# A two-block transformer kernel: order of the first loads, of two matmul halves, and the queue of three small loads

## The chip, the cores and the metric

One of the eight cores of a Trainium2 chip runs the whole program. The metric is the device time of one execution in microseconds. Engines are named as the profile names them: PE (TensorE, with PEld for its weight loads), ACT (ScalarE), DVE (VectorE), POOL (GpSimd), SP (SyncE, which here only issues transfers).

## The reference

Two transformer blocks follow one another on x of 256 tokens by 1024 features, float32. What matters here is the start of the first one:

```
def first_block(x, mem, positions, g_norm, w_in, ...):
    cos_a, sin_a = rope_tables(positions, A_ROT)
    cos_b, sin_b = rope_tables(positions, B_ROPE)
    for layer in range(DEPTH):
        h = rms_norm(x, g_norm[layer])
        proj = h @ w_in[layer]
        (q_a, k_a, v_a, q_i, k_i, w_i, z_a, c_q, c_kv, k_rope, z_b, q_m, z_m,
         gate_logits) = jnp.split(proj, split_at, axis=-1)
...
```

The projection feeds three attention branches (sparse top-k, latent, and cross attention to `mem`), each gated and projected, and a sum with x. The second block has a mixer (differential attention and gated linear attention), cross attention, and a mixture of 32 experts in 4 groups with two experts per token; the experts' weights alone are 201 MB.

## The kernel before, in words

**Products.** Every dense product is a `Job`: a matrix of weights cut in blocks of 128 rows, and up to 512 columns. `ORDER` (line 31) lists by hand in which order the jobs' halves (four blocks of rows each) are loaded and multiplied; it begins `c1 c2 c2 c1`, which are two parts of 336 columns each of `w_in`. `Stream` (line 102) walks through that list. `fetch` (line 128) takes a piece of memory and issues the load of the next half on SP's queue; `top_up` (line 146) fetches as long as fewer than `room` (6 at the start) loads are in flight and pieces are free. `split` (line 161) cuts a load into units of two blocks of rows (four for narrow products) and makes two float32r parts of each unit: ACT rounds it (line 165, the high part), DVE takes the remainder (line 166, the low part). `pump` (line 189) splits up to four units ahead and then issues a unit's matmuls (line 214).

**Three matmuls per block.** The left side, x transposed, is also kept as a high and a low part (`Left`, line 55). For each block `i` and each half `t` of the tokens, `pump` issues three matmuls, `c` = 0, 1, 2. Line 213 chooses the part of x, line 214 the part of the weights:

```
steps = [(i, t, c) for i in range(kb) for t in range(NT) for c in range(3)]
if 0:
    steps.sort(key=lambda s_: s_[2] == 2)
...
    x_ = j.X.at(k0 + off + i)[c == 0][:, t * P:(t + 1) * P]
    mm(j.outs[t], lhsT=x_, rhs=hl[:, int(c == 2), i, :], ...)
```

Index 0 is the high part, 1 the low part. So c = 0 is low x by high weights, c = 1 high by high, c = 2 high x by low weights.

**The start.** Lines 415 to 433 issue the first loads, all on SP's queue, in this order: columns 0 to 511 of x (512 KB, `load_x(0)`), the positions (line 421), three gain vectors (`g_norm`, `g_cq`, `g_ckv`, line 424), the first two halves of weights (`W.fetch()` twice, 672 KB each; called w0 of job c1 and w1 of job c2 here), columns 512 to 1023 of x, four short gain rows copied to all partitions (line 431), and then, from `top_up`, four more halves of weights. Seventeen more gain rows follow (line 459).

**The first products.** Line 706 runs seven small matmuls to keep TensorE busy (`keep_warm`). Line 708 transposes the gains. Line 713 transposes blocks 0 to 3 of x (line 543 on PE), and `split_evac` writes their high part on ACT (line 526) and their low part on DVE (line 527). Line 716 splits the first unit. Lines 718 to 741 are the rotary angles: POOL converts the positions (line 719) and reduces the angles (lines 729 to 739), ACT takes sine and cosine (line 740), POOL negates (line 741). Line 742 is the first `pump()`: it splits units two to four and issues the matmuls of the first unit. Line 743 transposes blocks 4 to 7 of x, and `pump(4)` in line 774 issues the next four units. Each engine works through its own instructions in the order in which they are issued here.

**The end.** The experts run in eight rounds of four; their weights come through the same pieces of memory (23 of 1 MB), and the loads follow as pieces come free.

Of the kernel before, what the change touches and what calls it, by code (L numbers as in the profile page):

```python
# [19 lines left out]
P = 128  # L20
# [17 lines left out]
ROWS = {}  # L38
# [63 lines left out]
class Stream:  # L102
# [25 lines left out]
    def fetch(self):  # L128
        src, _ = self.loads[self.next_load]
        w = self.k.take(list(src.shape))  # L130
        i, n, dma = self.next_load, len(self.loads), self.k.nc.sync.dma_start
        self.loads[i][1] = w
        self.next_load += 1
        if i < n - QUAD:
            dma(out=w, in_=src)
        elif i == n - 1:

            for c in range(2):
                for x in range(n - QUAD, n):
                    cuts = [slice(0, 4)] if (c, x) != (1, n - 1) else [slice(0, 2), slice(2, 4)]  # L140
                    for kb in cuts:
                        part = (slice(None), kb, slice(c * 256, c * 256 + 256))
                        dma(out=self.loads[x][1][part], in_=self.loads[x][0][part])  # L143
        self.flying += 1

    def top_up(self):
        splits = min(3 - len(self.hl), len(self.units) - self.next_split)
# [41 lines left out]
    def pump(self, n=1):  # L189
        for _ in range(n):  # L190
            self.top_up()
            if self.idle():
                self.flush()
                return
            self.split_ahead(4)
            u = self.next_mm
            j, _, k0, kb, off, last, _ = self.units[u]
            hl = self.hl.pop(u)
            if j.outs is None:
                j.outs = [self.k.ps([P, 512], "g")[:, :j.n] for _ in range(NT)]  # L200
            mm, ends = self.k.nc.tensor.matmul, {}

            steps = [(i, t, c) for i in range(kb) for t in range(NT) for c in range(3)]
            if 0:
                steps.sort(key=lambda s_: s_[2] == 2)
            if j.kb + kb == j.K:
                steps.sort(key=lambda s_: s_[1])
            for t in range(NT):
                mine = [s_ for s_ in steps if s_[1] == t]
                ends[t] = (mine[0] if j.kb == 0 else None, mine[-1] if j.kb + kb == j.K else None)  # L210
            for step in steps:
                i, t, c = step
                x_ = j.X.at(k0 + off + i)[c == 0][:, t * P:(t + 1) * P]
                mm(j.outs[t], lhsT=x_, rhs=hl[:, int(c == 2), i, :], start=step == ends[t][0], stop=step == ends[t][1])  # L214
            j.kb += kb
            self.k.give(1)
            if last:
                j.X.was_read(k0, off + kb)
            self.next_mm += 1
            if self.bg and next(self.bg, self) is self:  # L220
                self.bg = None
            self.flush()
            if j.kb == j.K:
                self.pending = j
# [9 lines left out]
class Kit:  # L234
# [15 lines left out]
    def ct(self, shape, name, dt=F32):  # L250
        n = int(np.prod(shape[1:]))
        if shape[0] == P and n <= 8 and dt in (F32, I32):

            if self.tiny is None:
                self.tiny = self.const.tile([P, 120], F32, name="tiny", tag="tiny")
            self.tiny_used += n
            ap = self.tiny[:, self.tiny_used - n:self.tiny_used]
            ap = ap.bitcast(dt) if dt != F32 else ap
            names = "abc"[:len(shape) - 1]
            return ap.rearrange(f"p ({' '.join(names)}) -> p {' '.join(names)}", **dict(zip(names, shape[1:])))  # L260
        return self.const.tile(shape, dt, name=name, tag=name)
# [9 lines left out]
    def ps(self, shape, tag, dt=F32):  # L271
        return self.psp.tile(shape, dt, name=self.name("p" + tag), tag=tag, bufs=self.BANKS[tag])
# [50 lines left out]
def block_kernel(ctx: ExitStack, tc: tile.TileContext, a: dict, out: bass.AP):  # L323
    k = Kit(tc, ctx)
    nc = tc.nc
    PE, ACT, DVE, POOL, SP = nc.tensor, nc.scalar, nc.vector, nc.gpsimd, nc.sync
# [15 lines left out]
    for i, br in enumerate("ABM"):  # L342
        for c in range(2):
            c0 = c * 512
            job(f"g{br}{c}", w_in[:, 4840 + i * D + c0:4840 + i * D + c0 + 512])
            job(f"w{br}{c}", a["w_branch"][0, i, :, c0:c0 + 512])
    for n, w, width in (("uq1", "w_uq", 384), ("uq2", "w_uq", 384), ("ukv1", "w_ukv", 512), ("ukv2", "w_ukv", 512)):
        c0 = width * (int(n[-1]) - 1)
# [19 lines left out]
    W = Stream(k, parts)  # L368
# [31 lines left out]
    for quad in range(32 // QUAD):  # L400
        both = [[f(QUAD * quad + i) for i in range(QUAD)] for f in (expert_srcs, packed_srcs)]
        for m in range(3):
            for half in range(2):
                W.add_loads([both[packed(quad, m)][i][m][half] for i in range(QUAD)])

    pump, need = W.pump, W.need


# [3 lines left out]
    rows0 = cut([13, P])  # L412
    h = ct([P, NT, D], "h")

    def load_x(half):
        SP.dma_start(out=h[:, :, half * 512:half * 512 + 512],
                     in_=a["x"][0, :, half * 512:half * 512 + 512].rearrange("(t p) c -> p t c", p=P))

    load_x(0)
    pos_i = ct([P, NT], "pos_i", I32)  # L420
    SP.dma_start(out=pos_i, in_=a["positions"].rearrange("o (t p) -> p (o t)", p=P))
    for name in ("g_norm", "g_cq", "g_ckv"):
        r, n = ROWS[name]
        SP.dma_start(out=rows0[r:r + n, :], in_=a[name].rearrange("o (k p) -> (o k) p", p=P))
    for _ in range(2):
        W.fetch()
    load_x(1)
    gbc = cut([P, 96])
    for off, src in ((64, a["g_kn_b"][:, 64:96]), (32, a["g_qn_b"][:, 64:96]),
                     (0, a["g_qn_a"][:, 0:16]), (16, a["g_kn_a"][:, 0:16])):  # L430
# [48 lines left out]
    def g_(name, i=0):  # L479
        c = ROWS[name][0] + i  # L480
        return gcol[:, c:c + 1]


    def keep_warm(n, size):

        for _ in range(n):
            PE.matmul(ps([P, size], "g"), lhsT=ident, rhs=h[:, 0, 0:size] if size > P else ident, start=True,
                      stop=True)
# [7 lines left out]
    def rstd_of(ss, n, shape):  # L496
        u, r = sm(*shape[1:]), sm(*shape[1:])
        DVE.tensor_scalar(u, ss, 1.0 / n, EPS, op0=OP.mult, op1=OP.add)  # L498
        power(r, u, shape)
        return r  # L500
# [23 lines left out]
    def split_evac(src, dstH, dstL, scale):  # L524

        ACT.activation(dstH, src, AF.Copy, scale=scale)
        DVE.scalar_tensor_tensor(dstL, src, scale, dstH.bitcast(F32), op0=OP.mult, op1=OP.subtract)
# [3 lines left out]
    def transposed(src, X, kbs, scales, first=0, tags=None, per=2):  # L531


        for g0 in range(0, len(kbs), 4):
            banks = []
            for k0 in range(g0, min(g0 + 4, len(kbs)), per):
                blk = kbs[k0:k0 + per]
                turn[0] += 1
                tp = ps([P, 2, S], tags[k0 // per] if tags else "sc" if turn[0] % 3 else "tp")
                for i, kb in enumerate(blk):  # L540
                    for t in range(NT):
                        c = (kb - first) * P
                        PE.transpose(tp[:, i, t * P:(t + 1) * P], src(t)[:, c:c + P], ident)  # L543
                banks.append((tp, blk))
            for i in range(2):
                for tp, blk in banks:
                    if i < len(blk):
                        split_evac(tp[:, i, :], *X.at(blk[i]), scales(blk[i]))
# [14 lines left out]
    def head_ss(src, heads, d):  # L563

        ss = sm(heads)
        per = 512 // d
        for h0 in range(0, heads, per):
            n = min(per, heads - h0)
            sq = st([P, n, d], "wk")
            ACT.activation(sq, src[:, h0:h0 + n, :], AF.Square)  # L570
            DVE.tensor_reduce(out=ss[:, h0:h0 + n], in_=sq, axis=AX.X, op=OP.add)
        return ss
# [36 lines left out]
    def pumps(counts):  # L609

        return lambda i: pump(counts[i])
# [84 lines left out]
    def silu2(dsts, srcs, half):  # L696
# [4 lines left out]
        for t in range(NT):  # L701
# [1 line left out]

    keep_warm(7, P)
    tp0 = ps([P, 13], "tp")
    PE.transpose(tp0, rows0, ident[0:13, 0:13])
    DVE.tensor_copy(gcol[:, 0:13], tp0)
    X1 = Left(k, 8)  # L710
    of_x = [J[n] for n in ("c1", "c2", "qi1", "qi2", "ka", "qa", "zb", "va", "qm", "za", "zm",
                           "gB0", "gB1", "gM0", "gM1", "gA0", "gA1")]
    transposed(lambda t: h[:, t, :], X1, list(range(4)), lambda kb: g_("g_norm", kb), tags=("sc", "sc", "tp", "o"),
               per=1)
    X1.read_by(of_x, 1)
    W.split_ahead(1)

    posf = ct([P, NT], "posf")
    POOL.tensor_copy(posf, pos_i)
# [12 lines left out]
    for cc in (C1, C2, C3):  # L732
# [11 lines left out]
               per=1)  # L744
# [652 lines left out]
    tp = ps([P, S], "tp")  # L1397
# [93 lines left out]
    for t in range(NT):  # L1491
# [21 lines left out]
        r = rstd_of(head_ss(og, 4, 128), 128, [P, 4])  # L1513
# [547 lines left out]
```

## Time and profile before

| | |
|---|---|
| median of 3 runs | 1033.25 us (1033.2 to 1033.74) |
| the profiled execution, its own time | 1033.29 us |
| its span, first to last instruction | 1031.6 us |
| PE busy | 913.9 us (89%) |
| DVE busy | 445.4 us (43%) |
| ACT busy | 333.1 us (32%) |
| POOL busy | 113.8 us (11%) |
| moved by DMA | 289.85 MB, mean 281 GB/s |
| mean granted clock of TensorE | 0.965 |

The times of rows are microseconds from the span's start. In rows of the timeline the first number is the start, the second how long it took, and in brackets stands the idle time of that engine before it and what ended it. The granted clock is a share of full speed: 1.00 is 2.4 GHz and 0.50 is 1.2 GHz.

### The profile page before, as it was taken

The numbers are of one execution on the slowest core, as the hardware profiler recorded it, in microseconds if no ns is written. First come the engines' busy times: TensorE is split into PE (matmuls) and PEld (weight loads), VectorE is DVE, ScalarE is ACT, GpSimd is POOL, SyncE is SP. The second block draws the span as 40 slices with busy tenths as digits, with TensorE's granted clock in tenths as the row PEclk, the third lists the DMA queues.
The fourth block names the chain that finished last, engine by engine and source line by source line (L and its number), as shares of the span: only waits on it lengthen the run. The fifth ranks groups of instructions, "written<-read, shape, count | busy, mean of one in ns | idle before, by whom it ended". The sixth has DMA issues, their size and how long they took to land.

```text
span 1031.6 us, 12785 instructions
## 1 busy us (share of the span) xinstructions
PE 913.9 (89%) x5053; PEld 614.3 (60%) x5053; DVE 445.4 (43%) x814; ACT 333.1 (32%) x637; POOL 113.8 (11%) x156
## 2 busy tenths in 40 slices
PE   8999999999999999999999998968777786786766
PEld 8978887888788887877878752414142141423223
DVE  5689775776767565767756411101000010100002
ACT  6556665555445472556553200000000000000000
POOL 4354100120222020310011000000000000000000
PEclk9999999999999999999999999989899898989989
DMA  7943346354564723553687899999999999999997
GB/s 223 385 131 123 94 154 202 123 189 139 164 209 130 240 87 123 179 188 124 218 331 232 327 400 418 420 420 419 420 420 419 420 420 419 420 419 421 419 408 244
DMA packets 88316, 289.85 MB, mean 281 GB/s; under 512 B 5841, under 2 KB 20030, under 8 KB 66750
## 3 DMA queue, kind: packets, MB, share of 16 engines
q1 hardware_dynamic: 87150, 286.33, 73.4%
q0 software_dynamic: 960, 2.55, 1.0%
q8 instruction: 41, 0.67, 0.3%
q14 instruction: 21, 0.17, 0.0%
q10 hardware_dynamic: 144, 0.13, 0.0%
HBM read 287.94 MB, written 1.05 MB: 280 GB/s over the span
## 4 chain that ended last, share of the span: by engine, by line
PE 49%; DMA 38%; DVE 8%; ACT 2%; SPq 1%; issue 1%; POOL 0%; ACTq 0%; POOLq 0%; DVEq 0%
PE pg L214 36%; DMA s<-in_w_e_up_dram 13%; DMA s<-in_w_e_down_dram 12%; DMA s<-in_w_e_gate_dram 12%; DVE s L166 2%; PE po L675 2%; PE psc L1871 2%; PE psc L543 1%; ACT s L628 1%; DVE s L577 1%; PE ptp L638 1%; PE psc L1905 1%; PE psc L1641 1%; SPq L143 1%; PE ptp L1828 1%
## 5 line engine op out<-in xcount | busy, mean ns | idle before, releaser
L214 PE MATMUL pg<-s,s 128*128 128x512 f32 (+5 forms) x2076 | 454.2, 376 | 5.3 <-ACT s L165 2.0
L214 PEld LDWEIGHTS pg<-s,s 128*128 128x128 f32 x2076 | 365.2, 189 | 72.7 <-issue 3.3
L1871 PE MATMUL psc<-s,wk 128*32 128x512 f32 (+1 forms) x1024 | 175.9, 683 | 65.1 <-DMA s<-in_w_e_up_dram 40.6
L166 DVE TENSOR_TENSOR s<-s,s 128x1024 fp32r<-128x1024 f32 (+4 forms) x170 | 196.9, 1190 | 45.8 <-ACT s L165 45.6
L165 ACT ACTIVATE s<-s 128x1024 fp32r<-128x1024 f32 (+4 forms) x170 | 160.6, 995 | 13.1 <-DVE s L166 7.6
L1871 PEld LDWEIGHTS psc<-s,wk 128*32 128x32 f32 x1024 | 41.0, 125 | 192.8 <-issue 75.6
L1905 PE MATMUL psc<-s,wk 128*32 128x512 f32 (+1 forms) x576 | 71.5, 559 | 12.8 <-DMA s<-in_w_e_down_dram 12.3
L1878 DVE SCALAR_TENSOR_TENSOR wk<-wk,psc 128x512 f32<-128x512 f32 x8 | 5.5, 688 | 134.2 <-ACT wk L1877 134.2
L1895 ACT ACTIVATE wk<-ptp 128x512 f32<-128x512 f32 (+1 forms) x9 | 4.9, 550 | 171.2 <-PE ptp L1894 171.2
L1882 DVE TENSOR_TENSOR wk<-wk,psc 128x512 f32<-128x512 f32 (+1 forms) x8 | 5.2, 654 | 119.5 <-PE psc L1871 119.5
L494 POOL TENSOR_TENSOR sm<-sm,tiny 128x8 f32<-128x8 f32 (+2 forms) x28 | 36.0, 1298 | 171.6 <-DVE sm L498 142.3
L1905 PEld LDWEIGHTS psc<-s,wk 128*32 128x32 f32 x576 | 19.8, 112 | 58.2 <-issue 31.9
L628 ACT ACTIVATE s<-psc,sm,tiny 128x256 f32<-128x256 f32 (+1 forms) x64 | 32.8, 523 | 60.4 <-DVE sm L625 59.9
L1828 PE MATMUL ptp<-masks,h 128*128 128x128 f32 x128 | 30.2, 392 | 12.7 <-DVE masks L1815 12.7
L1828 PEld LDWEIGHTS ptp<-masks,h 128*128 128x128 f32 x128 | 28.6, 311 | 19.1 <-issue 17.5
L1877 ACT ACTIVATE wk<-psc 128x512 f32<-128x512 f32 x8 | 4.8, 597 | 108.3 <-PE psc L1871 108.3
L1910 DVE COPY wk<-psc 128x512 f32<-128x512 f32 (+1 forms) x10 | 6.1, 612 | 60.2 <-PE psc L1905 60.2
L1917 PE MATMUL pg<-wk,wr 128*128 128x512 f32 (+1 forms) x72 | 30.4, 561 | 0.5 <-DVE wk L1910 0.5
L1828 PE MATMUL po<-masks,h 128*128 128x128 f32 x120 | 28.2, 388 | 0.0
L624 DVE TENSOR_REDUCE sm<-psc 128x2 f32<-128x512 f32 (+1 forms) x26 | 17.9, 688 | 23.9 <-PE psc L1198 8.1
L1912 ACT ACTIVATE wk<-psc 128x512 f32<-128x512 f32 (+1 forms) x8 | 4.6, 570 | 73.1 <-PE psc L1905 73.1
L1828 PEld LDWEIGHTS po<-masks,h 128*128 128x128 f32 x120 | 27.6, 319 | 0.0
(329 smaller groups left out, 784.1 us busy)
## 6 DMA issues: line engine op xcount, KB each, us to landing
s<-in_w_e_gate_dram SPq DMA_DIRECT2D x64, 1024.0 KB
s<-in_w_e_up_dram SPq DMA_DIRECT2D x64, 1024.0 KB
s<-in_w_e_down_dram SPq DMA_DIRECT2D x60, 1024.0 KB
s<-in_w_in_dram SPq DMA_DIRECT2D x36, 1024.0 KB
s<-in_w_ckv_dram SPq DMA_DIRECT2D x8, 1024.0 KB
s<-in_w_branch_dram SPq DMA_DIRECT2D x6, 1024.0 KB
s<-in_w_mem_kv_dram SPq DMA_DIRECT2D x4, 1024.0 KB
s<-in_w_out_dram SPq DMA_DIRECT2D x4, 1024.0 KB
```

The lines of the kernel that those rows point to most:

```text
L143: dma(out=self.loads[x][1][part], in_=self.loads[x][0][part])
L165: self.k.nc.scalar.activation(hl[:, 0], w, AF.Copy)
L166: self.k.nc.vector.tensor_tensor(out=hl[:, 1], in0=w, in1=hl[:, 0].bitcast(F32), op=OP.subtract)
L214: mm(j.outs[t], lhsT=x_, rhs=hl[:, int(c == 2), i, :], start=step == ends[t][0], stop=step == ends[t][1])
L494: POOL.tensor_tensor(out=dst, in0=src, in1=e_.to_broadcast(shape), op=OP.pow)
L624: DVE.tensor_reduce(out=mx, in_=sc, axis=AX.X, op=OP.max)
L628: ACT.activation(e[:, i, :], sc[:, i, :], AF.Exp, bias=nb[:, i:i + 1], scale=rs[:, c:c + 1], accum_out=sums[:, c:c + 1])
L675: PE.matmul(o[:, hd % (out_heads or heads), :], lhsT=pt[:, i * nkt + kt, :], rhs=vals(kt, hd), start=(kt == 0), stop=(kt == nkt - 1))
L1828: PE.matmul(tp[:, kb - k0, :], lhsT=src, rhs=sel[:, t], start=(t == 0), stop=(t == 1))
L1871: PE.matmul(p_[s0:s0 + sn, :], lhsT=xs[k0 // 4][:, kb, s0:s0 + sn], rhs=rows(m, i, k0 + kb, cols), start=(k0 + kb == 0), stop=(k0 + kb == 7))
L1905: PE.matmul(p_[s0:s0 + sn, :], lhsT=hT[:, kb, s0:s0 + sn], rhs=rows(2, i, kb, slice(c * 512 + cols.start, c * 512 + cols.stop)), start=(kb ...
L1917: PE.matmul(outs[t][c], lhsT=sgT[:, t, :], rhs=od, start=start, stop=stop)
```

## The change

The first loads are issued in another order and in other pieces: columns 0 to 255 of x, the first two blocks of w0, columns 256 to 511 of x, the last two blocks of w0, w1, columns 512 to 1023 of x, and then the positions. The loads of the three gain vectors go to ACT's queue. `fetch` takes the piece for the first load, but leaves its transfers to the caller. Seven matmuls of `keep_warm` become five. Blocks 0 to 3 of x are transposed in two pairs, with the split of the first unit between them. In every unit c = 0 is now high by high and c = 1 low x by high weights, and the first unit does all its products with the weights' high part before those with the low part.

```diff
@@ fetch
         self.next_load += 1
+        self.flying += 1
+        if i == 0:
+            return
         if i < n - QUAD:
             dma(out=w, in_=src)
...
-        self.flying += 1
@@ pump
-            if 0:
+            if u == 0:
                 steps.sort(key=lambda s_: s_[2] == 2)
...
-                x_ = j.X.at(k0 + off + i)[c == 0][:, t * P:(t + 1) * P]
+                x_ = j.X.at(k0 + off + i)[c == 1][:, t * P:(t + 1) * P]
@@ block_kernel
-    def load_x(half):
-        SP.dma_start(out=h[:, :, half * 512:half * 512 + 512],
-                     in_=a["x"][0, :, half * 512:half * 512 + 512].rearrange("(t p) c -> p t c", p=P))
-
-    load_x(0)
+    def load_x(c0, n):
+        SP.dma_start(out=h[:, :, c0:c0 + n], in_=a["x"][0, :, c0:c0 + n].rearrange("(t p) c -> p t c", p=P))
+
+    for name in ("g_norm", "g_cq", "g_ckv"):
+        r, n = ROWS[name]
+        ACT.dma_start(out=rows0[r:r + n, :], in_=a[name].rearrange("o (k p) -> (o k) p", p=P))
+    W.fetch()
+    for b in range(2):
+        load_x(b * 256, 256)
+        SP.dma_start(out=W.loads[0][1][:, 2 * b:2 * b + 2], in_=W.loads[0][0][:, 2 * b:2 * b + 2])
+    W.fetch()
+    load_x(512, 512)
     pos_i = ct([P, NT], "pos_i", I32)
     SP.dma_start(out=pos_i, in_=a["positions"].rearrange("o (t p) -> p (o t)", p=P))
-    for name in ("g_norm", "g_cq", "g_ckv"):
-        r, n = ROWS[name]
-        SP.dma_start(out=rows0[r:r + n, :], in_=a[name].rearrange("o (k p) -> (o k) p", p=P))
-    for _ in range(2):
-        W.fetch()
-    load_x(1)
     gbc = cut([P, 96])
@@ block_kernel
-    keep_warm(7, P)
+    keep_warm(5, P)
...
-    transposed(lambda t: h[:, t, :], X1, list(range(4)), lambda kb: g_("g_norm", kb), tags=("sc", "sc", "tp", "o"),
-               per=1)
+    transposed(lambda t: h[:, t, :], X1, [0, 1], lambda kb: g_("g_norm", kb), tags=("sc", "sc"), per=1)
     X1.read_by(of_x, 1)
     W.split_ahead(1)
+    transposed(lambda t: h[:, t, :], X1, [2, 3], lambda kb: g_("g_norm", kb), tags=("tp", "o"), per=1)
```

## Rows read from the trace of the kernel before

**Rows 1.** The page: the chain by engine, and the costliest group of instructions.

```profile
PE 49%; DMA 38%; DVE 8%; ACT 2%; SPq 1%; issue 1%; POOL 0%; ACTq 0%; POOLq 0%; DVEq 0%
...
L214 PE MATMUL pg<-s,s 128*128 128x512 f32 (+5 forms) x2076 | 454.2, 376 | 5.3 <-ACT s L165 2.0
```

**Rows 2.** The chain in order of time, 0 to 50 us: start, duration, what.

```profile
8.03 0.77 ACT s L165
...
9.73 3.17 PE pg L214 x10
...
13.96 14.52 PE pg L214 x96
...
29.57 17.51 PE pg L214 x120
```

**Rows 3.** The timeline of all engines, 0 to 20 us.

```profile
4.73 0.19 POOL L719 CAST tiny<-tiny 128x2 f32<-128x2 int32 x1 [2.93 <-DMA tiny<-in_positions_dram]
...
5.92 0.90 ACT L526 ACTIVATE s<-psc,gcol 128x256 fp32r<-128x256 f32 x2 [3.61 <-PE psc L543]
...
8.84 0.57 PE L214 MATMUL pg<-s,s 128*128 128x336 f32 x2 [2.02 <-ACT s L165]
...
10.58 0.26 ACT L740 ACTIVATE s<-s 128x64 f32<-128x64 f32 x1 [1.80 <-POOL s L739]
10.75 2.06 ACT L165 ACTIVATE s<-s 128x672 fp32r<-128x672 f32 x3
...
11.53 2.40 DVE L166 TENSOR_TENSOR s<-s,s 128x672 fp32r<-128x672 f32 x3 [1.85 <-ACT s L165]
```

**Rows 4.** The timeline of SP's queue, 0 to 12 us, from several windows.

```profile
0.82 0.44 SPq L416 DMA_DIRECT2D h<-in_x_dram  x1
1.32 0.45 SPq L421 DMA_DIRECT2D tiny<-in_positions_dram  x1
...
3.85 0.50 SPq L416 DMA_DIRECT2D h<-in_x_dram  x1
...
8.02 0.38 SPq L135 DMA_DIRECT2D s<-in_w_in_dram  x1
...
11.25 0.37 SPq L135 DMA_DIRECT2D s<-in_w_in_dram  x1
```

**Rows 5.** Waits of SP's queue, 0 to 12 us: total, times, longest.

```profile
SPq L135 <- DMA s<-in_w_in_dram: 2.0, 2, 1.5
SPq L135 <- DMA h<-in_x_dram: 1.0, 1, 1.0
```

**Rows 6.** Windows of 1 us: busy time by engine, PEclk, DMA share, GB/s last.

```profile
2.00:3.00 1.00, 1.00 (x7) 1.00 (x6) 0.00 (x0) 0.30 (x2) 0.00 (x0) 1.00 0.88 217
3.00:4.00 1.00, 1.00 (x7) 1.00 (x7) 0.00 (x0) 0.00 (x0) 0.00 (x0) 1.00 0.96 302
4.00:5.00 1.00, 0.80 (x4) 0.52 (x4) 0.00 (x0) 0.00 (x0) 0.19 (x1) 1.00 0.84 122
...
8.00:9.00 1.00, 0.16 (x1) 0.16 (x2) 0.30 (x2) 0.76 (x1) 0.75 (x4) 1.00 1.08 397
```

**Rows 7.** Windows of PE alone: length, busy, PEclk, DMA share, GB/s.

```profile
6.85:8.80 1.95, 0.00 (x0) 1.00 1.07 388
...
9.75:13.10 3.35, 3.35 (x12) 0.50 0.99 300
13.10:17.00 3.90, 3.90 (x29) 0.99 1.08 367
```

**Rows 8.** Waits of PE and of ACT, whole span.

```profile
PE pg L214 <- DVE s L527: 1.1, 2, 0.7
...
ACT s L165 <- DMA s<-in_w_in_dram: 0.5, 1, 0.5
```

**Rows 9.** Windows of 4 us at the first experts, columns as in rows 6.

```profile
588.00:592.00 4.00, 4.00 (x39) 1.97 (x42) 2.52 (x14) 0.35 (x2) 0.00 (x0) 1.00 0.09 35
...
600.00:604.00 4.00, 4.00 (x44) 1.04 (x32) 0.00 (x0) 0.00 (x0) 0.00 (x0) 1.00 1.02 426
```

## The prediction

> **What bounds the kernel now.** I read the page's chain first: TensorE and the weight transfers carry nearly all of the span [rows 1]. The change touches only the start, so the next view is the chain in order of time over the first 50 us [rows 2]. The reader is to see that the kernel's first 14 us hang on one transfer: ScalarE can round the first block of weights (w0, L165) only when it has landed, at 8.03; ten matmuls of the first unit run until 12.9, transposes follow, and from 13.96 TensorE runs 96 matmuls without a gap, and 120 more until 47. So what counts is when the second unit starts; in that row it is 13.96.
>
> The timeline of ScalarE, VectorE and GpSimd shows a second chain beside it [rows 3]. GpSimd converts the positions when they have landed (4.73), works out the angles, and ScalarE's sine L740 starts at 10.58, after an idle wait. Behind that sine, in ScalarE's order, stand the splits of units two to four (L165 x3, from 10.75). Now the second unit's split is done about 2 us before TensorE wants it. That is all the slack that the positions have.
>
> The view of SyncE's queue shows in which order transfers are issued and, by its waits, when they land [rows 4, 5]. Positions are the second transfer, and land right behind the first half of x. w0 is in at 8.02, where the queue's wait ends, as does ScalarE's. The second half of x, issued at 3.85, lands only at 11.25: the issue there waited 1.0 us for it. So a transfer that fills half a megabyte lands over 7 us behind its issue, and after w0, which was issued ahead of it.
>
> **The change, part by part.**
>
> *First loads by quarters.* x columns 0 to 255, half of w0, x 256 to 511, the other half of w0, w1, and then the second half of x go out back to back at some 0.47 us each, from 0.82. The first unit needs the first two of them only, about half of what stood ahead of it. Its split can start near 6 instead of 8.03, a gain of about 2 us for that unit. It isn't counted: the second unit stands behind the sine.
>
> *Positions behind all of x.* This is the term that decides. In SyncE's order 2.43 MB now stand ahead of the positions (1.05 MB of x, 1.38 MB of w0 and w1). Their issue ends near 4.1. The trace has no such transfer behind so much, so its landing, T, is bounded. Same bytes, same queue: the second half of x, the last of these, landed at 11.25 [rows 4]. Before, the three microseconds to 5.0 moved 217, 302 and 122 KB, 0.64 MB in all [rows 6]. With the large transfers back to back I estimate 1.0 MB by then (217, then two at the best row's rate), which at 390 GB/s saves 0.9 us: 10.35. The positions' own 256 four-byte pieces add some 0.5, as in the slow fifth microsecond: **T = 10.8**. Lower end: 2.43 MB at the best row's 397 GB/s from 2.0 on are through at 8.1, and 0.7 for the small pieces: 8.8. Upper end: nothing saved, 11.25 and the same 0.7: 12.0. I take 10.8, nearest to the landing of the same bytes.
>
> From T on, the rows give durations: GpSimd's chain 4.73 to 10.58, 5.85 us; sine to the next split 0.17; split to the first matmul 0.81 (8.03 to 8.84 for the first unit) [rows 2, 3]. So the second unit starts at T + 6.83. It is level with the old start where T = 13.96 - 6.83 = 7.1. With T = 10.8 it starts at 17.6, **3.7 us later** (ends: 1.7 and 4.9).
>
> *The clock.* After the idle stretch from 6.85 to 8.80 the granted clock was 0.50 from 9.75 to 13.10, while TensorE worked without a gap, and 1 again behind that [rows 7]. In the new order TensorE would finish the first unit near 9, transpose the second half of x near 11, and stand idle some 5 us until 17.6. I expect one such spell to fall on the second unit. Its price: ten matmuls took 3.17 us in the spell and 96 took 14.52 us outside, 0.317 against 0.151 each; 3.35 us of it is 10.6 matmuls, times 0.166, **1.75 us**. Ends: nothing (the clock is up when the unit starts) and two spells, 3.5. I take one, as the trace shows one after an idle time shorter than this. The spell of before lay on the old path too, but ahead of 13.96, so it is not to be given back.
>
> *Units begin with the high parts.* Per unit, matmul one now needs only ScalarE's halves. That saves at most one matmul where TensorE waits for L527: two waits, 1.1 us in all [rows 8], of which two matmuls of some 0.23 us can move up: **-0.4 us**. On the new second unit it does not avoid the wait for L166: two matmuls can run, 0.63 us at the half clock, of 0.80 that the remainder takes (2.40 for three [rows 3]): **+0.2**. The number of matmuls and weight loads stays, so elsewhere it costs nothing below or above.
>
> *The rest.* Gain rows on ScalarE's queue: three issues of 0.25 to 0.4 us ahead of ScalarE's first work, covered by its idle time until 5.92 [rows 3]; without that cover they would cost 0.9 us of ScalarE. Two warming matmuls fewer: about 1 us of TensorE before any data is there, nothing. Transposes in two pairs: the same eight. The four small gain loads and the next four weight blocks follow the positions on SyncE; their first use is unit five, 36 matmuls behind the second, so 1 us either way is hidden. ScalarE's later work moves by 6.1 us (10.58 to 16.65), its evacuations of x's second half too; the fifth unit's split would end near 21.5, and TensorE, itself late, asks for it near 25.
>
> *Does the delay reach the end?* ScalarE waits for a weight transfer once, at the first unit [rows 8]; no later wait of that kind could absorb it. The expert weights stop at 588 to 592 (share 0.09), with every buffer full, until TensorE frees some, and then run at 420 GB/s [rows 9] as far as the last ones. Their restart moves with TensorE, so the delay is passed on whole.
>
> Sum: 3.7 + 1.75 + 0.2 - 0.4 = **+5.2 us**. The profiled execution took 1033.29 us, 0.04 over the median, so the sum is made against it: **1038.5 us**.
>
> **The rivals.** 0.2% is 2.1 us, about what a measurement of this kernel tells from no change.
>
> (a) *Positions overtake* (not slower; decides at T = 7.1). They land at the delay seen before, 2.96 us after the end of their issue (1.77 to 4.73): T = 7.1. The second unit then starts level, and with -0.4 the time is 1032.9; with a spell of the half clock it is 1034.6. For it: the transfer is tiny. Against it: the second half of x stayed behind w0, though it was issued 4 us before w0 was in [rows 4]. The Trainium skill (DMA: Bandwidth & Descriptors, Queues, rings and completion order) says that completion is not first-in first-out per issuing engine, a later small transfer may finish first; by that rule alone the sum would be that of this rival. It also says that each of the transfer engines takes descriptors in ring order, which is what these rows look like. Chance 0.09.
>
> (b) *Late, but at full clock.* 3.7 + 0.2 - 0.4 = +3.5: 1036.8. For it: the clock was 1 through the idle time itself and fell only 0.9 us after it. Against it: the idle time is more than twice as long. Chance 0.12.
>
> (c) *The high parts pay everywhere.* All waits in front of L214 come to 5.3 us [rows 1], 2.3 at the first unit, so 3.0 is the most that the order could win; with the second unit level, 1030.3. It needs T near 7 as well. Chance 0.08.
>
> (d) *Absorbed.* Past 60 us other work than TensorE's sets the pace, and slack there takes all but 1 us: 1034.3. Against it, the chain runs on through TensorE from 13.96, with no gap, to 47 [rows 2]. Chance 0.05.
>
> That the first unit doesn't start sooner is no case of its own, as the sum doesn't rest on it.
>
> **How the numbers follow.** The forecast has 0.66. Its own ends: 1.7 + 0 + 0.2 - 0.4 = +1.5 (1034.8) and 4.9 + 3.5 + 0.2 - 0.4 = +8.2 (1041.5). The range goes from 1034.0, which takes in (b) and (d), to 1041.5; (a) and (c), 0.17, are left out. Slower by over 0.2% is forecast and (b), 0.78; within 0.2% (a) and (d), 0.14; faster (c), 0.08.
>
> **What would show it.** Right: the positions' conversion (L719) near 10.8, the sine near 16.6 after a wait of 8 us or so of ScalarE, the first unit of L214 near 7, its second near 17.6, the granted clock at 0.5 behind that, and 588 to 594 moved by about 5 us. Wrong: L719 before 7.1, or ScalarE's splits ahead of the sine; then (a). A clock of 1 from 17.6 on means (b). A second unit at 17.6 with the expert weights restarting at the old time means (d).

## The result, and the profile after

The changed kernel takes 1037.82 us (median of 6 runs, 1036.33 to 1040.6) against 1033.28 before (6 runs): a ratio of 1.0052, with a 95% interval of 1.004 to 1.0063. It is slower by 4.5 us; 5.2 were forecast. The profiled execution took 1037.53 us, with a span of 1035.5.

Lines behind line 130 stand two or three further down now: L214 is L216, L165 is L167, L719 is L722, L740 is L743, L135 is L138.

The timeline of all engines of the changed kernel, 7 to 17 us, answers [rows 3]:

```profile
7.28 3.73 PE L216 MATMUL pg<-s,s 128*128 128x336 f32 x12
...
10.63 0.19 POOL L722 CAST tiny<-tiny 128x2 f32<-128x2 int32 x1 [8.84 <-DMA tiny<-in_positions_dram]
...
14.88 0.35 POOL L739 TENSOR_SCALAR s<-s 128x32 f32<-128x32 f32 x1
...
15.93 0.26 ACT L743 ACTIVATE s<-s 128x64 f32<-128x64 f32 x1 [7.98 <-POOL s L742]
16.09 2.05 ACT L167 ACTIVATE s<-s 128x672 fp32r<-128x672 f32 x3
```

The first unit starts 1.6 us sooner than before. The positions are converted at 10.63 instead of 4.73, ScalarE waits 8.0 us in front of its sine, and the second unit's split comes out behind it. The chain in order of time shows what that makes of the second unit and of what follows, against [rows 2]:

```profile
16.89 17.03 PE pg L216 x96
...
35.01 17.52 PE pg L216 x120
```

It starts at 16.89, 2.93 us late; its 96 matmuls take 17.03 us instead of 14.52; and from there the same work takes the same time, 17.52 against 17.51. So a loss of 5.44 us is made before 34 us; what comes behind that takes some of it back. The windows of TensorE alone (length, busy time, granted clock, DMA share, GB/s), as [rows 7], show the second part of it:

```profile
6.85:8.80 1.95, 1.81 (x7) 1.00 1.07 403
12.00:14.80 2.80, 0.03 (x1) 0.96 1.07 367
14.80:21.30 6.50, 4.41 (x14) 0.50 0.38 125
21.30:25.00 3.70, 3.70 (x25) 0.98 0.63 184
```

TensorE stands idle from 12 on, the clock falls to 1.2 GHz near 14.7, and comes back near 21.3, after 4.4 us of work at half speed. The 1.00 of the first row is not borne out by the work: seven matmuls take 1.81 us there and the first unit's twelve 3.73, 0.31 each, as at 0.50 (14 in 4.41) and not as at 0.98 (25 in 3.70). So TensorE most likely ran the first unit at half speed too; this trace has no record of the clock ahead of 11.2 us. At the other end, the transfers of the experts stop and start again some 4 us later than in [rows 9]:

```profile
588.00:592.00 4.00, 2.57 (x18) 1.55 (x16) 2.57 (x17) 0.00 (x0) 0.00 (x0) 1.00 1.00 410
592.00:596.00 4.00, 4.00 (x41) 2.38 (x43) 2.67 (x13) 0.35 (x2) 0.00 (x0) 1.00 0.21 82
```

### The profile page after: what moved, and what is told of

It reads as the page before. It is cut to its first block, busy times and chain, and to the rows that moved or that the text cites. A ratio compares the mean times of both kernels' runs of the same rounds, so it can differ in the third digit from the quotient of the medians.

```text
span 1035.5 us, 12783 instructions
## 1 busy us (share of the span) xinstructions
PE 914.9 (88%) x5049; PEld 616.7 (60%) x5049; DVE 445.3 (43%) x814; ACT 332.9 (32%) x637; POOL 113.2 (11%) x156
## 4 chain that ended last, share of the span: by engine, by line
PE 51%; DMA 37%; DVE 6%; issue 2%; ACT 2%; SPq 1%; POOL 1%; ACTq 0%; POOLq 0%; DVEq 0%
PE pg L216 37%; DMA s<-in_w_e_up_dram 13%; DMA s<-in_w_e_down_dram 12%; DMA s<-in_w_e_gate_dram 12%; PE po L678 2%; PE psc L1874 2%; DVE s L168 2%; PE psc L546 1%; PE ptp L641 1%; PE psc L1644 1%; PE psc L1908 1%; ACT s L631 1%; SPq L146 1%; PE ptp L1831 1%; DVE s L580 1%
## 5 line engine op out<-in xcount | busy, mean ns | idle before, releaser
L216 PE MATMUL pg<-s,s 128*128 128x512 f32 (+5 forms) x2076 | 456.9, 377 | 7.0 <-ACT s L167 4.9
L216 PEld LDWEIGHTS pg<-s,s 128*128 128x128 f32 x2076 | 367.3, 190 | 75.4 <-ACT s L167 5.6
L1874 PE MATMUL psc<-s,wk 128*32 128x512 f32 (+1 forms) x1024 | 171.2, 655 | 65.8 <-DMA s<-in_w_e_up_dram 43.0
L167 ACT ACTIVATE s<-s 128x1024 fp32r<-128x1024 f32 (+4 forms) x170 | 160.6, 995 | 12.6 <-DVE s L168 7.6
L1908 PE MATMUL psc<-s,wk 128*32 128x512 f32 (+1 forms) x576 | 73.4, 560 | 13.3 <-DMA s<-in_w_e_down_dram 13.0
```

The lines of the kernel that those rows point to most:

```text
L167: self.k.nc.scalar.activation(hl[:, 0], w, AF.Copy)
L1874: PE.matmul(p_[s0:s0 + sn, :], lhsT=xs[k0 // 4][:, kb, s0:s0 + sn], rhs=rows(m, i, k0 + kb, cols), start=(k0 + kb == 0), stop=(k0 + kb == 7))
L1908: PE.matmul(p_[s0:s0 + sn, :], lhsT=hT[:, kb, s0:s0 + sn], rhs=rows(2, i, kb, slice(c * 512 + cols.start, c * 512 + cols.stop)), start=(kb ...
```

## The experiments

The theory: late positions hold ScalarE's sine, the sine holds the splits behind it, TensorE waits and then works cold. Its rivals were that the pieces of the loads or the other queue cost the time themselves, or that late positions do by some other way. Every kernel was run in five rounds beside the kernel before.

**e1, the positions on ScalarE's queue.**

```diff
     for name in ("g_norm", "g_cq", "g_ckv"):
         r, n = ROWS[name]
         ACT.dma_start(out=rows0[r:r + n, :], in_=a[name].rearrange("o (k p) -> (o k) p", p=P))
+    pos_i = ct([P, NT], "pos_i", I32)
+    ACT.dma_start(out=pos_i, in_=a["positions"].rearrange("o (t p) -> p (o t)", p=P))
...
-    pos_i = ct([P, NT], "pos_i", I32)
-    SP.dma_start(out=pos_i, in_=a["positions"].rearrange("o (t p) -> p (o t)", p=P))
```

> The changed kernel, with the positions alone issued on ScalarE's queue behind the three gain vectors. Theory (positions late, ScalarE's sine holds the second unit's split): L719's counterpart starts near 5 instead of 10.6, the sine near 10.5, and the second unit of matmuls starts near 12, when blocks 4 to 7 of x are transposed (11.7 to 12.0 in the changed kernel), not at 16.9; the granted clock stays at 1 from 12 on; the time is 1033.3 - 2 (12 against 13.96) - 0.7 (high parts first), 1030.6, within 1029.5 to 1032. Rival (the pieces of the first loads, or the other queue for the gains, cost the 4.5 us themselves): the second unit stays near 17 and the time at 1037 to 1038.

Measured: 1032.57 us, ratio 1.0003 (0.9992 to 1.0014). The loss is gone, so neither the pieces of the loads nor the other queue for the gains cost it. The gain that I expected on top is not there: the time lies above my range, and cannot be told from that of the kernel before. Its timeline:

```profile
6.06 0.19 POOL L722 CAST tiny<-tiny 128x2 f32<-128x2 int32 x1 [4.27 <-DMA tiny<-in_positions_dram]
...
6.94 0.66 PE L546 MATMUL ptp<-ident,h 128*128 128x128 f32 x2 [0.92 <-DMA h<-in_x_dram]
...
11.88 0.26 ACT L743 ACTIVATE s<-s 128x64 f32<-128x64 f32 x1 [3.34 <-POOL s L742]
...
12.84 0.58 PE L216 MATMUL pg<-s,s 128*128 128x336 f32 x2 [0.22 <-ACT s L167]
```

The positions land a microsecond later than I had put them; why is not shown. TensorE also waits 0.92 for x's second quarter, but that need not come of the positions: its transposes start at 6.94 here, at 6.49 in e7 with the same loads, and at 5.97 to 6.67 in the five kernels that have these loads with the positions behind x. The sine at 11.88 still holds the second unit, to 12.84, and then it waits for VectorE's remainder until 13.74.

**e2, the sine behind the splits, the positions still late.**

```diff
-    ACT.activation(cs[:, :, 0:2, :], ang, AF.Sin)
-    POOL.tensor_scalar(cs[:, :, 2, :], cs[:, :, 1, :], -1.0, None, op0=OP.mult)
     pump()
...
     W.split_ahead(3)
+    ACT.activation(cs[:, :, 0:2, :], ang, AF.Sin)
+    POOL.tensor_scalar(cs[:, :, 2, :], cs[:, :, 1, :], -1.0, None, op0=OP.mult)
```

> The changed kernel, with the sine and the negation behind it moved in ScalarE's and GpSimd's order behind the splits of units two to four and the evacuations of blocks 4 to 7; the positions stay late. Theory: positions still land at 10.6 and the sine runs near 16, but the second unit starts near 12 as the splits no longer stand behind the sine; the fifth unit's split follows the sine at 16.1 and is done at about 16.9, when TensorE wants it (12 + 36 x 0.151 = 17.4), so the time is that of e1, 1030.6, up to 0.5 us more. Rival (late positions cost by their own chain, through the rotary tables or the scale of the first products, wherever the sine stands): 1036 or more.

Measured: 1030.3 us, ratio 0.9979 (0.997 to 0.9988). This one separates the theories: the positions are as late as in the changed kernel, and nothing is lost. Its timeline:

```profile
8.91 1.42 ACT L167 ACTIVATE s<-s 128x672 fp32r<-128x672 f32 x2 [0.33 <-DMA s<-in_w_in_dram]
...
10.77 0.61 POOL L722 CAST tiny<-tiny 128x2 f32<-128x2 int32 x1 [8.98 <-DMA tiny<-in_positions_dram]
...
11.44 5.77 PE L216 MATMUL pg<-s,s 128*128 128x336 f32 x36
...
16.56 0.26 ACT L749 ACTIVATE s<-s 128x64 f32<-128x64 f32 x1 [3.92 <-POOL s L742]
...
18.41 8.97 PE L216 MATMUL pg<-s,s 128*128 128x336 f32 x58 [0.31 <-DVE s L168]
```

The splits run from 8 on, the second unit starts at 11.44 (the transposes of x's second half end there), and only the fifth unit waits a little for the sine at 16.56.

**e3, the kernel before with the positions alone moved.**

```diff
-    pos_i = ct([P, NT], "pos_i", I32)
-    SP.dma_start(out=pos_i, in_=a["positions"].rearrange("o (t p) -> p (o t)", p=P))
...
     load_x(1)
+    pos_i = ct([P, NT], "pos_i", I32)
+    SP.dma_start(out=pos_i, in_=a["positions"].rearrange("o (t p) -> p (o t)", p=P))
```

> The kernel before, with one part of the change alone: the positions are issued behind the second half of x. Theory: they land near 11.5 to 12 (the second half of x landed at 11.23), the sine starts near 17.1, the second unit near 18 instead of 13.96, cold for some 4 us: 1033.3 + 4.1 + 2.3 = 1039.7, within 1037.5 to 1041. Rival (small transfers overtake, or the old order has slack that the new one lost): within 1 us of 1033.3.

Measured: 1038.56 us, ratio 1.0058 (1.0043 to 1.0072). This one part of the change, alone, loses as much as the whole. Two rows of its timeline:

```profile
16.64 0.26 ACT L740 ACTIVATE s<-s 128x64 f32<-128x64 f32 x1 [8.26 <-POOL s L739]
...
17.60 16.92 PE L214 MATMUL pg<-s,s 128*128 128x336 f32 x96 [4.54 <-ACT s L165]
```

And one of its windows, of TensorE alone, at the half clock:

```profile
18.00:20.00 2.00, 2.00 (x7) 0.50 0.07 23
```

**e4 and e5, the clock.** Matmuls of the identity fill TensorE's wait, ten in e4, 22 in e5.

```diff
     W.split_ahead(3)
+    J["c2"].outs = [ps([P, 512], "g")[:, :J["c2"].n] for _ in range(NT)]
+    for _ in range(22):
+        PE.matmul(J["c2"].outs[0][:, 0:P], lhsT=ident, rhs=ident, start=True, stop=True)
```

> The changed kernel, with ten matmuls of the identity (each 0.48 us at half the clock and 0.5 or less at full) put behind the transposes of blocks 4 to 7, into banks that the second job clears later: work that is added, none is left out. Theory: in the changed kernel the granted clock was 0.5 from 14.8 to 21.3 and cost 96 matmuls 17.03 us in place of 14.52; here it stays at 1 through the second unit, the 96 matmuls take 14.5 to 15, and the time falls by 2 to 2.5 us from 1037.8, to 1035.5. Rival (the matmuls are slow for another reason, as a split that feeds them late): no change, or 1 us slower.

Measured: 1038.6 us, ratio 1.0057 (1.0044 to 1.007), no gain. The timeline says why:

```profile
11.94 2.40 PE L753 MATMUL pg<-ident 128*128 128x128 f32 x20
17.45 0.58 PE L216 MATMUL pg<-s,s 128*128 128x336 f32 x2 [3.12 <-ACT s L167]
18.35 16.03 PE L216 MATMUL pg<-s,s 128*128 128x336 f32 x94 [0.31 <-DVE s L168]
```

At full clock the ten were through in 2.4 us, half of what I had allowed for. TensorE was idle for 3.1 us again, and 94 matmuls took 16.03 us: the half clock only came later. So e4 settled nothing, and e5 fills the whole wait.

> As e4, with 22 added matmuls instead of ten: e4's ten ran at full clock, took 2.4 us and left TensorE idle for 3.1 us again, and the clock fell near 19. 22 of them take some 5.3 us, from 12 to 17.3, as long as the second unit has to wait. Theory (the clock is one term of the delay, 96 matmuls in 17.03 us instead of 14.5): the granted clock stays at 1 from 12 to 34, the 96 take at most 15.2, TensorE comes to the first transposes behind them at 32 instead of 33.9, and the time falls by 1.5 to 2.5 us, to 1035.3 to 1036.3. Rival (the split feeds the unit late): no change, or slower by the added work.

Measured: 1034.93 us, ratio 1.002 (1.0011 to 1.003), 2.9 us under the changed kernel, and more than I expected.

Its timeline:

```profile
12.00 5.08 PE L753 MATMUL pg<-ident 128*128 128x128 f32 x44
17.22 0.57 PE L216 MATMUL pg<-s,s 128*128 128x336 f32 x2
18.11 14.49 PE L216 MATMUL pg<-s,s 128*128 128x336 f32 x94 [0.32 <-DVE s L168]
```

The same 94 in the changed kernel, by their weight loads, which start with the matmuls here:

```profile
17.79 15.90 PEld L216 LDWEIGHTS pg<-s,s 128*128 128x128 f32 x94 [0.39 <-DVE s L168]
```

The second unit starts 0.3 us later than in the changed kernel, and 94 matmuls take 14.49 us, with the clock at 1 (the windows from 12 to 24 us all have 1.00), where the changed kernel's run from 17.79 to 33.92, 16.13 us. So the clock was a term of its own, of 1.6 us. The 2.9 us of the medians are more than this trace shows: TensorE is 1.3 us ahead of the changed kernel at 33.7 us and 0.6 at 395, and the execution that was profiled, 1036.81 us, was the slowest of the eleven. Where the rest comes from is not shown.

**e6, the kernel before with the high parts first alone** (the two lines of `pump`, as in the change).

> The kernel before, with the order of the matmuls alone (line 213, and the sort in the first unit). Theory: each unit that waits for the low part of x starts one matmul sooner; by the offsets of the changed kernel's trace this is worth 0.4 us between 165 and 230 and 0.3 us between 250 and 390, so 0.7 us, 1032.5, with the first 50 us the same to within 0.3. Rival (the order pays in every unit): 3 us, 1030.

Measured: 1030.81 us, ratio 0.9981 (0.997 to 0.9991), three times what I expected. Part of it is plain. The first unit, with the products that need the weights' low part behind the others, no longer waits for VectorE:

Its timeline:

```profile
8.60 3.00 PE L214 MATMUL pg<-s,s 128*128 128x336 f32 x12 [1.84 <-ACT s L165]
...
12.93 14.77 PE L214 MATMUL pg<-s,s 128*128 128x336 f32 x96
```

Before, two matmuls ran at 8.84, and ten from 9.73 to 12.9 [rows 2, 3]; here all twelve are through at 11.6, and TensorE is 0.8 us ahead at 50 us. At 390 us it is 1.5 ahead: 0.4 more come at 208 to 216, where the kernel before waits for the transfer of `mem`, and 0.23 near 325. What comes behind that moves with stretches of the half clock further on, and is not settled.

**e7, e1 and e2 together.**

> e1 and e2 together: the positions on ScalarE's queue, and the sine behind the splits and evacuations. Theory: in e2 the fifth unit still waits for the sine (TensorE idle at 17.5 and 18.1, and its first two matmuls spread over 0.9 us); here the sine is ready near 11.9 and no unit waits, TensorE runs 96 matmuls without a gap from 11.5 to 12.6 on and is through at 26 to 27.1 against 27.4: 0.3 to 1.4 us faster than e2's 1030.3, 1028.9 to 1030.0. Rival (positions on the other queue cost the large loads what they save): 1030.3 to 1031.5.

Measured: 1030.29 us, ratio 0.9978 (0.9966 to 0.999), level with e2.

Its timeline:

```profile
11.66 14.77 PE L216 MATMUL pg<-s,s 128*128 128x336 f32 x96
```

No unit waits any more, as expected, and these 96 are through at 26.43, in e2 at 27.38. In the medians that lead doesn't show: see the last section. e2 and e7 have the lowest medians of the study, and are faster than the kernel before and the changed one by more than their intervals; e6, half a microsecond above them, is not told apart.

**e8, the old order of the loads, with the sine behind the splits and the high parts first.**

> The loads of the kernel before, with the sine behind the splits and the high parts first: what e2 has without the new order of the loads. Theory: in the kernel before nothing stood behind the sine for long, so moving it gains nothing; the first unit waits for w0 until 8, its matmuls run at half the clock, the second unit starts within 0.3 of 13.96, and the time is that of e6, 1032.5. The new order of the loads is then worth the difference to e7, some 3 us. Rival (what made e2 faster was the sine, not the loads): 1030 to 1031.

Measured: 1031.29 us, ratio 0.9989 (0.9978 to 1). It is level with e6, as expected: before the change nothing stood behind the sine for long. The new order of the loads would be worth the difference to e7, 1.0 us and not 3, and the two intervals do not tell that from nothing: with the high parts first the old order's second unit starts at 12.80, counted as the 13.96 is, and not near 13.96 as I had put it. In the traces e7 is 0.9 us ahead of e8 at the next 120 matmuls (27.52 against 28.42), and e2, with the new order and late positions, is level with e8 (28.47).

**e9, the changed kernel with the matmuls in the old order.**

> The changed kernel with the order of the matmuls as before (both lines), all else changed. Theory: what the high parts first are worth adds to the rest: without them the 96 matmuls end within 0.5 us of 33.9, TensorE is 0.4 us later between 165 and 230 and 0.3 us later between 250 and 390, and the time is 0.7 us (their steady part) to 2.2 us (all that e6 gained) above 1037.8, 1038.5 to 1040. Rival (e6 gained by the place of the clock's spells alone): 1037.8 within 0.5, and no offset that grows between 165 and 390.

Measured: 1038.21 us, ratio 1.0051 (1.0038 to 1.0065), no difference from the changed kernel that this measurement can tell (the ratios to the kernel before are 1.0051 and 1.0052; by their intervals some 2 us either way would be hidden, and e9 ran on another chip than the other experiments). The trace shows a steady part, though. The longest waits of TensorE for this line (total, times, longest) in e9, and below them those in the changed kernel:

```profile
PE pg L216 <- ACT s L167: 4.9, 1, 4.9
PE pg L216 <- DVE s L530: 1.1, 2, 0.7
```

```profile
PE pg L216 <- ACT s L167: 4.9, 1, 4.9
PE pg L216 <- ACT s L918: 1.1, 1, 1.1
```

The two waits for the low part of x, 1.1 us, are gone with the high parts first. At their places, near 325 and 497 us, the changed kernel gains 0.22 and 0.23 us on this one. The 0.4 that I expected between 165 and 230 is not there: e9 makes up 0.43 on the kernel before at 208 to 216, as the changed kernel does. And its 96 matmuls end at 34.7, not within 0.5 of 33.9, as the positions are converted only at 11.42 in this execution.

## Why the prediction was right

*The positions' landing.* Right, and the term that decided, with some luck in the number. T was put at 10.8 and came out at 10.63. The second half of x was to land at 10.35; SyncE's queue issues the next load at 10.36, in its timeline, and its view of waits (total, times, longest) says that it had waited for x:

```profile
10.36 0.93 SPq L138 DMA_DIRECT2D s<-in_w_in_dram  x2
```

```profile
SPq L138 <- DMA h<-in_x_dram: 1.2, 1, 1.2
```

The small transfer landed 0.3 us behind the large ones and overtook nothing, which ends rival (a). The Trainium skill (DMA: Bandwidth & Descriptors, Queues, rings and completion order) says that descriptors of one ring are taken in order, and that completion need not be; here the trace agrees with the first and shows nothing of the second. The same page (Issuing engines are not separate DMA queues) says that transfers run on the same DMA engines and interleave, whichever engine issues them; no run here shows that apart: positions from the other queue landed at 6.06 in e1 and 6.58 in e7, and x's second quarter came within the scatter named under e1 in e7, and 0.3 us behind it in e1.

The luck is this. The 10.35 for x counted on 1.0 MB by 5.0 us. The changed kernel's windows, columns as in [rows 6], show 0.77, against 0.64 before:

```profile
2.00:3.00 1.00, 1.00 (x7) 1.00 (x6) 0.00 (x0) 0.95 (x1) 0.00 (x0) 1.00 0.84 256
3.00:4.00 1.00, 0.94 (x5) 0.65 (x4) 0.00 (x0) 0.53 (x2) 0.00 (x0) 1.00 0.99 276
4.00:5.00 1.00, 0.23 (x2) 0.23 (x2) 0.00 (x0) 0.00 (x0) 0.00 (x0) 1.00 1.00 238
```

At 390 GB/s that is 0.3 us of the 0.9 that x gained; the rest was won later, where the kernel before had its slow microsecond (176 KB from 10 to 11). And with the same loads in the same order the conversion came at 10.63 here, 10.77 in e2, 10.97 in e5, 11.21 in e4 and 11.42 in e9, so that an agreement within 0.2 is closer than the executions agree with each other.

*From the positions to the second unit.* 5.85 us were taken from the rows for GpSimd's chain, and 5.30 measured. The difference is one operation: it took 0.91 us before (L736 there) and 0.35 here (L739, shown above). Before, it began at 8.97, behind the start of a remainder on VectorE (L166, 8.82 to 9.68), and ended 0.2 behind that remainder's end; now VectorE has none there. So the second unit was 2.93 us late and not 3.7. The term was mis-sized because a duration was carried over from a busier stretch; the last section has more of these.

*The clock.* 1.75 us and 0.2 for the remainder's wait were put down, 2.51 measured (17.03 - 14.52). e5 parts the two. Behind the remainder's wait the clock cost 1.64 us (94 matmuls in 16.13 instead of 14.49), near the 1.75. The other 0.87 lies at the head of the unit, where 0.2 was put down, and this term was mis-sized: the third matmul starts 0.90 us behind the first, where two take 0.30 at full clock. Most of the remaining 0.27 is in the counting: the chain counts the old unit from 13.96, and its first matmul starts at 13.71 in the timeline. That the clock's price came out is in part luck, as the spell was twice as long as the 3.35 that I took (14.7 to 21.3) and 2.2 us of it passed while TensorE still waited. Rival (b) falls, as the clock stood at 0.50 from 14.8 to 21.3.

*High parts first.* -0.4 was put down, one matmul at each of two waits, and it came out: in every kernel that has the high parts first TensorE gains 0.22 to 0.24 us on the kernel before near 325 us and 0.23 to 0.25 near 497, and in e3 and e9, which have not, no more than 0.02 at either place. What e6 showed, 0.8 us in the first unit, could not count here, as the first unit isn't on the path any more. Rival (c) falls with the landing, as it needed T near 7. Its 3 us over all units are not seen in any trace.

*The delay reaches the end.* Nearly. The delay was 5.4 us at 57, 5.4 at 165, 5.0 at 233 and 4.7 at 395, and the first expert matmuls start at 593.77 against 589.15, 4.6 us late; the last results are added 4.4 us later (1031.03 against 1026.62). The 0.4 between 165 and 233 goes with the transfer of `mem`, which stood in the chain of before (5.75 us from 209.99 on, and TensorE waited for it) and doesn't in that of the changed kernel; this was read from the chains and not tried. It is not lateness absorbed, as (d) would have it: e3, 6.0 us late, still waits for `mem` and gains nothing there, and e6, 0.8 us early, gains the same 0.4. What decides it is open. 0.5 are the high parts, as forecast. So the 5.2 of the forecast became 4.4 at the end of this trace, and 4.5 in the medians: 0.8 less for the start of the second unit, 0.6 more for the clock with the head of the unit, 0.4 made up at `mem`, and 0.2 in small differences.

## What to carry to other kernels

An early transfer that is tiny can be worth more than the large one that takes its place: before moving a load, follow what waits for it, and what stands behind that waiting instruction on its own engine. Here 1 KB of positions held a 0.26 us sine, and the sine held three splits that needed none of it; moving the sine by a few lines (e2) made the late load free. And when an early wait is opened on TensorE, add the clock to its price: here a wait of 4.9 us was followed by 4.4 us of work at 1.2 GHz, which cost some 1.6 us more.

## What was not expected

*Places of the half clock far from the change.* Near 410 us TensorE waits 1.2 us and 0.4 us for VectorE, in every kernel. In some traces the clock falls there and in others not. The window of 396 to 420 us of TensorE alone, in the kernel before, in e2, in e7 and in e6:

```profile
396.00:420.00 24.00, 22.49 (x123) 0.93 0.28 90
```

```profile
396.00:420.00 24.00, 22.49 (x130) 1.00 0.35 115
```

```profile
396.00:420.00 24.00, 22.49 (x122) 0.93 0.30 95
```

```profile
396.00:420.00 24.00, 22.49 (x123) 0.93 0.29 95
```

When the kernel arrives does not decide it: e2 and e6 both come there 1.49 us ahead of the kernel before, with the same waits, and the clock falls in e6 alone.

e2 is 1.5 us ahead of the kernel before at 400 us and 3.1 ahead at 460; e7 is 2.3 ahead at both. So e2 gains there more than e7 had won at the start. A second place is near 540 us: in the profiled run of e2 the clock was 0.83 from 530 to 540, in e7's it was up, and there e7 takes the lead again (4.0 against 3.2 us at 568). Over all runs the two end level. In these traces such a place is worth 1.5 us. They may be what spreads the runs of one kernel as well (e7: 1027.75 to 1032.54), which is not shown, as one execution of each kernel was traced. A gain of a microsecond at the start of this kernel can so vanish or double by the end, and how much of e6's 2.2 us is steady was left open for this reason.

*The cost of a shared stretch.* The same GpSimd operation on 128x32 took 0.91 us beside a remainder on VectorE and 0.35 alone. It is the remainder that counts, and not any work of VectorE's: beside the evacuations of L527 GpSimd's operations before took 0.25 to 0.29 us, as they do alone. In e1 another one met a remainder, and took 0.85 where it takes 0.31 in the changed kernel (L734 at 11.96):

```profile
7.22 0.86 DVE L168 TENSOR_TENSOR s<-s,s 128x672 fp32r<-128x672 f32 x1 [0.17 <-ACT s L167]
7.39 0.85 POOL L734 TENSOR_SCALAR s<-s 128x32 f32<-128x32 f32 x1
```
